# Two decoder layers on one core: later constants, one-step token shift, two-pass sums in RWKV, three-pass LRU gates, whole blocks in the output projections

## The chip, the core and the metric

The kernel runs on one core of a Trainium2 chip. The core has the engines TensorE (PE), VectorE (DVE), ScalarE (ACT), GpSimd (POOL) and SyncE (SP), an on-chip memory of 128 partitions and matmul banks that sum in float32. The metric is the device time of one execution in microseconds (us).

## What is computed

A trunk of two layers on a sequence of T = 256 tokens with D = 2048 columns, in float32. Cut to what matters here:

```python
for layer in range(2):
    h = rms_norm(x, norm_mix[layer])
    if layer == 0:                       # sparse attention beside RWKV-7
        u_nsa, u_rw = split(h @ w_in_a)
        y = concat([nsa(u_nsa), rwkv7(u_rw)]) @ w_out_a
    else:                                # RG-LRU beside HGRN2
        u_lru, u_hg = split(h @ w_in_b)
        y = concat([rglru(u_lru), hgrn2(u_hg)]) @ w_out_b
    x = x + y
    x = x + square(relu(rms_norm(x, norm_mlp[layer]) @ w_ff1)) @ w_ff2

# in rwkv7
u = u + (u_prev - u) * mu                # token shift, u_prev is u one token earlier
kk = k * k_k; kk = kk / max(sqrt(sum over a head's 64 columns of kk*kk), 1e-12)
bonus = (sum over a head's 64 columns of r * k * r_k) * v
# in rglru, for each of 8 blocks of 128 columns
r = sigmoid(xc_block @ wa_block + ba);  i = sigmoid(xc_block @ wx_block + bx)
h_t = a_t * h_(t-1) + b_t                # a from r, b from r, i and xc
y = h * gelu(gate_in)
```

## The kernel before

Activations lie transposed: 16 tiles of 128 columns by 256 tokens. Products are made of float32 values that are cut in two: a rounded high part (type fp32r in the profile) and the rest, the low part. An operand tile holds both beside each other, 512 columns. For each of 16 k, `mm3` (L156) multiplies the high weights with the 512 columns (L163) and the low weights with the 256 high columns (L164); the two halves of the bank are added when it is emptied (`evac`, L175). This pair is called a k below. In the *folded* form the 512 columns are two matmuls of 256 into the same half (L160, L161), so that no adding is left. One 2048 x 128 block of weights times 256 tokens is a *unit*: 16 k.

Weights come as float32 in halves of 8 k (tile `raw`, pool `wraw` with 4 buffers, loads issued by SP in `load`, L135). `split` (L139) makes the high part by a CAST on ACT (`wh`, L141) and the low part by a subtraction on DVE (`wl`, L143); each has 2 buffers in the pool `wspl`.

The program order is: six units of the input projection that run k by k beside each other while x and the weights arrive (tiles `hx_a`, `wh_i_f`, `wl_i_f`; then the mean square `ms_a` with a matrix of ones), then `rwkv_a` with units 6 to 27, the solve, `nsa_head` eight times, the output projection (`mm_o`), the MLP (`mm_f`), and the same with `hgrn_head` and `lru_group` for layer 1. A scheduler sets the order on each engine from the order in which the code is written and from priorities (`tc.high_priority`, `tc.issue_after`).

`con` holds constant matrices (identity, `bones` for sums over 64 rows, `ones`, tables). It is loaded by SP among the loads of the first stage (L283). `out_proj` (L972) goes over one half of the inputs for all 16 output blocks c, and then over the other half in the folded form, after which block c is complete and `touch` (L238) makes the next operand and its sum of squares. In layer 1 the half that comes second is LRU's, whose inputs `ym[0..7]` are the last to be ready: at the end of `lru_group` each of four goes through Exp on ACT (L964), two products, a scan and a product on DVE (L965 to L968), a CAST on ACT (L193) and a subtraction on DVE (L194).

## Time and profile before

| what | value |
|---|---|
| time, median of 3 runs | 2360.75 us (2359.98 to 2374.69) |
| time of the profiled execution | 2360.99 us |
| its span in the trace | 2359.2 us |
| granted TensorE clock, mean | 0.999 |
| first six units, first to last real matmul | 7.16 to 45.5 us |
| output projection, layer 0 | 412.5 to 520 us |
| output projection, layer 1 | 1549.5 to 1645 us |

The profiled execution is 0.24 us above the median and has 1.8 us outside its span. In the rows below a line is the line of the kernel before, `out<-in` the names of the tiles, and square brackets hold the idle time of the engine ahead of the instruction and what ended it. The duration of a matmul overlaps the next one, so the cost of a matmul is the distance between starts.

### The profile page before, as it was taken

To read this page: it belongs to the slowest core of one execution; us is meant where nothing else is said; L and a number is where in the kernel's file an instruction comes from. 1 tells how busy PE (TensorE), PEld (TensorE's weight loads), DVE (VectorE), ACT (ScalarE), POOL (GpSimd) and SP (SyncE) were. 2 spreads that over 40 slices of the span, in tenths; PEclk is the share of its full clock that TensorE was granted. 3 is DMA by queue.
4 is the path that set the end of the run, shared out by engine and by line. 5 is a ranking of instruction groups with operands and counts; after the bars stand their busy time and mean duration, and the time that the engine had idled before them with its cause. 6 is when DMAs were issued, how large, how long until landed. Compare 5 with 4: busy or idle time off the path is not lost.

```text
span 2359.2 us, 38438 instructions
## 1 busy us (share of the span) xinstructions
PE 2349.7 (100%) x14530; PEld 2061.7 (87%) x14530; DVE 1707.4 (72%) x3063; ACT 1252.2 (53%) x2178; POOL 78.6 (3%) x176
## 2 busy tenths in 40 slices
PE   9999999999999999999999999999999999999999
PEld 8888888898888888888888888889888888888888
DVE  6987878777775675675678888788777567567555
ACT  6755467554444444444456665775444444444443
POOL 0112142000000000000000000000000000000000
PEclk9999999999999999999999999999999999999999
DMA  7676754555555555555555444456555555555664
GB/s 245 211 260 230 242 168 137 202 182 192 189 188 192 191 188 189 193 189 188 190 171 181 155 152 153 160 170 215 188 191 191 189 189 191 191 189 189 191 198 137
DMA packets 128296, 445.72 MB, mean 189 GB/s; under 512 B 14960, under 2 KB 21232, under 8 KB 126960
## 3 DMA queue, kind: packets, MB, share of 16 engines
q1 hardware_dynamic: 114768, 407.77, 53.4%
q0 software_dynamic: 8944, 32.00, 4.0%
q10 hardware_dynamic: 4400, 3.50, 0.5%
q8 instruction: 115, 1.88, 0.3%
q14 instruction: 69, 0.57, 0.1%
HBM read 427.99 MB, written 15.20 MB: 188 GB/s over the span
## 4 chain that ended last, share of the span: by engine, by line
PE 83%; DVE 2%; ACT 1%; issue 1%; DMA 0%; POOL 0%; DVEq 0%; ACTq 0%; POOLq 0%
PE mm_f L163 39%; PE mm_f L164 21%; PE mm_i L163 8%; PE mm_i L164 4%; PE mm_o L164 2%; PE mm_o L163 2%; PE mm_o L160 1%; PE mm_o L161 1%; PE hl L872 1%; DVE wl_i L143 1%; DVE wl_o L143 0%; PE psu L541 0%; PE o L752 0%; PE psx L534 0%; ACT wh_o L141 0%
## 5 line engine op out<-in xcount | busy, mean ns | idle before, releaser
L143 DVE TENSOR_TENSOR wl_f<-raw_f,wh_f 128x1024 fp32r<-128x1024 f32 x512 | 627.5, 1226 | 472.2 <-ACT wh_f L141 470.7
L141 ACT CAST wh_f<-raw_f 128x1024 fp32r<-128x1024 f32 x512 | 539.7, 1054 | 758.4 <-PE mm_f L163 559.8
L163 PE MATMUL mm_f<-hx_m,wh_f 128*128 128x512 f32 x2048 | 710.5, 391 | 0.0
L163 PE MATMUL mm_f<-z,wh_f 128*128 128x512 f32 x2032 | 704.7, 391 | 0.0
L164 PE MATMUL mm_f<-hx_m,wl_f 128*128 128x256 f32 x2048 | 573.8, 280 | 0.0
L164 PE MATMUL mm_f<-z,wl_f 128*128 128x256 f32 x2032 | 569.0, 280 | 0.0
L163 PE MATMUL mm_i<-hx_a,wh_i 128*128 128x512 f32 x1440 | 526.1, 403 | 0.2 <-DVE s_r L179 0.2
L163 PEld LDWEIGHTS mm_f<-hx_m,wh_f 128*128 128x128 f32 x2048 | 383.0, 187 | 84.0
L163 PEld LDWEIGHTS mm_f<-z,wh_f 128*128 128x128 f32 x2032 | 380.0, 187 | 83.3
L164 PE MATMUL mm_i<-hx_a,wl_i 128*128 128x256 f32 x1440 | 416.9, 289 | 0.0
L164 PEld LDWEIGHTS mm_f<-hx_m,wl_f 128*128 128x128 f32 x2048 | 387.1, 189 | 0.1
L164 PEld LDWEIGHTS mm_f<-z,wl_f 128*128 128x128 f32 x2032 | 384.0, 189 | 0.0
L163 PEld LDWEIGHTS mm_i<-hx_a,wh_i 128*128 128x128 f32 x1440 | 270.7, 188 | 55.9 <-issue 0.7
L141 ACT CAST wh_i<-raw_i 128x1024 fp32r<-128x1024 f32 x180 | 189.2, 1051 | 176.2 <-PE mm_i L163 152.4
L164 PEld LDWEIGHTS mm_i<-hx_a,wl_i 128*128 128x128 f32 x1440 | 272.1, 189 | 4.8 <-DVE wl_i L143 1.3
L143 DVE TENSOR_TENSOR wl_i<-raw_i,wh_i 128x1024 fp32r<-128x1024 f32 x180 | 220.1, 1223 | 65.2 <-ACT wh_i L141 64.1
L179 DVE TENSOR_TENSOR s_f<-mm_f,t_f 128x256 f32<-128x256 f32 x255 | 106.7, 418 | 0.0
L143 DVE TENSOR_TENSOR wl_o<-raw_o,wh_o 128x1024 fp32r<-128x1024 f32 x64 | 78.3, 1223 | 30.0 <-ACT wh_o L141 29.5
L141 ACT CAST wh_o<-raw_o 128x1024 fp32r<-128x1024 f32 x64 | 67.2, 1050 | 61.2 <-issue 31.1
L178 ACT COPY t_f<-mm_f 128x256 f32<-128x256 f32 x255 | 92.8, 364 | 0.0
L164 PE MATMUL mm_o<-ym,wl_o 128*128 128x256 f32 x256 | 72.7, 284 | 0.9 <-DVE wl_o L143 0.9
L1011 DVE TENSOR_TENSOR s_f<-s_f,rstd_m 128x256 f32<-128x256 f32 x128 | 54.4, 425 | 4.4
(463 smaller groups left out, 2449.7 us busy)
## 6 DMA issues: line engine op xcount, KB each, us to landing
raw_f<-in_w_ff_dram SPq DMA_DIRECT2D x512, 512.0 KB, 4.5
raw_i<-in_w_in_dram SPq DMA_DIRECT2D x180, 512.0 KB, 4.0
raw_o<-in_w_out_dram SPq DMA_DIRECT2D x64, 512.0 KB, 4.4
rwp_d<-rwp POOLq DMA_DIRECT2D x8, 1024.0 KB, 5.4
raw_i_f<-in_w_in_dram SPq DMA_DIRECT2D x16, 384.0 KB, 4.7
pm_d<-pm POOLq DMA_DIRECT2D x8, 512.0 KB, 5.1
cw<-in_cmp_w_dram POOLq DMA_DIRECT2D x2, 2048.0 KB, 17.4
pmc<-pm_d POOLq DMA_DIRECT2D x8, 512.0 KB, 4.5
```

What stands on the lines that cost most here:

```text
L141: A.copy(wh, raw)
L143: V.tensor_sub(wl, raw, wh)
L160: M.matmul(ps[:, :T], wh, mv[:, :T], start=first, stop=False)
L161: M.matmul(ps[:, :T], wh, mv[:, T:], start=False, stop=False)
L163: M.matmul(ps, wh, mv, start=first, stop=False)
L164: M.matmul(ps[:, :T], wl, mv[:, :T], start=False, stop=last)
L178: A.copy(t, ps[:, T:])
L179: V.tensor_add(s, ps[:, :T], t)
L872: M.matmul(pl[:, x * T + i * P : x * T + (i + 1) * P], qk[:, ii], qk[:, ii], start=True, stop=True)
L1011: V.tensor_mul(s, s, rstd)
```

## The change

- `con` loses `ones` (1696 columns to 1568), which is set on the chip, and its load moves behind the loads of unit 6. The load of `par` is cut in two.
- Token shift: u + (u_prev - u) mu is written as u_prev mu + u (1 - mu). The product u (1 - mu) is made on ACT, and one DVE operation is left.
- The two sums over heads in `rwkv_a` (`kss`, `bon`, eight of each) go from one float32 matmul to two in fp32r, with the operand cut in two parts first.
- The LRU gates (16 matmuls) go from float32 to the folded `mm3`; their weights and their operand are cut in two.
- `out_proj` gets a number `nh`: the blocks c >= nh are made whole, 16 k in one bank, between the first halves and the folded halves of the blocks c < nh. It is 8 in layer 0 and 12 in layer 1, so there are 8 + 12 = 20 folded halves in place of 32.
- The reciprocal root for the MLP is placed by hand behind the ninth k of its first unit.

```diff
@@ -36,7 +36,7 @@
 _CON = [
-    ("ident", 128), ("bones", 128), ("ones", 128), ("pair", 128),
+    ("ident", 128), ("bones", 128), ("pair", 128),
     ("ropec", 256), ("ropes", 256), ("reset", 256), ("zd", 256), ("cadd", 32), ("cmul", 32),
@@ -92,7 +92,8 @@
     A.preload_act_table_set(LN_EXP)
-    nc.scalar.dma_start(par, params)
+    nc.scalar.dma_start(par[:, 0:64], params[:, 0:64])
+    nc.scalar.dma_start(par[:, 64:], params[:, 64:])
@@ -102,7 +103,9 @@
-    ident, bones, ones = c_("ident"), c_("bones"), c_("ones")
+    ident, bones = c_("ident"), c_("bones")
+    ones = cst.tile([P, P], F32, name="ones")
+    V.memset(ones, 1.0)
     epst = cst.tile([P, 4], F32, name="epst")
@@ -279,8 +289,6 @@
                         raws.append(raw)
-                        if k == 9:
-                            nc.sync.dma_start(con, consts)
                     for i in range(16):
@@ -306,9 +314,11 @@
                     rstd = rstd_of(acc, "a0", "gc")
+                first.append(unit(w_in0[NFIRST], hx, f"i0_{NFIRST}", tag="gb"))
+                with tc.high_priority(), tc.issue_after(last_load[0].ins):
+                    nc.sync.dma_start(con, consts)
                 A.copy(ones_r, ones)
                 A.copy(bones_r, bones)
-                first.append(unit(w_in0[NFIRST], hx, f"i0_{NFIRST}", tag="gb"))
                 rwkv_a(pa, gate, hx, scaled_by(rstd), rwp_d, pm_d, wts, nb, first, load_cw, anchor)
@@ -335,14 +345,16 @@
         mixed = [None]
+        keep = tl("keep", (P, 28))
+        V.tensor_scalar(keep, p_("mu"), -1.0, 1.0, op0=ALU.mult, op1=ALU.add)
...
             d = tl("d", bufs=2, name=f"d_{name}")
-            V.tensor_sub(d[:rows], ub[:rows, 0:T], ub[:rows, 1:])
-            mixed[0] = V.scalar_tensor_tensor(out[:rows], d[:rows], p_("mu", mu)[:rows], ub[:rows, 1:], ALU.mult, ALU.add)
+            A.activation(d[:rows], ub[:rows, 1:], AF.Copy, scale=keep[:rows, mu : mu + 1])
+            mixed[0] = V.scalar_tensor_tensor(out[:rows], ub[:rows, 0:T], p_("mu", mu)[:rows], d[:rows], ALU.mult, ALU.add)
             return ub
@@ -407,7 +419,10 @@
                 pss = bk_(f"kss_{j}")
-                M.matmul(pss[:, :T], bones, sq, start=True, stop=True)
+                hl = pa.tile([P, 2, T], F32R, tag="hl", name=f"khl_{j}")
+                A.activation(hl[:, 0], k, AF.Square, scale=p_("k_k", j))
+                V.tensor_sub(hl[:, 1], sq, hl[:, 0])
+                sum_over(pss[:, :T], bones_r, hl[:, 0], hl[:, 1])
                 ssm = tl("tm", bufs=2, name=f"ssm_{j}")
@@ -428,7 +443,10 @@
                 psb = bk_(f"bon_{j}")
-                M.matmul(psb[:, :T], bones, rk, start=True, stop=True)
+                hl = pa.tile([P, 2, T], F32R, tag="hl", name=f"bhl_{j}")
+                A.copy(hl[:, 0], rk)
+                V.tensor_sub(hl[:, 1], rk, hl[:, 0])
+                sum_over(psb[:, :T], bones_r, hl[:, 0], hl[:, 1])
                 bv = tl("kf", name=f"bv_{j}")
@@ -761,8 +779,12 @@
             nc.scalar.dma_start(hgmk, hgmask)
-            lw = hp.tile([P, 2, 8, P], F32, name="lw")
-            nc.scalar.dma_start(lw, lru_w)
+            lwh, lwl = (hp.tile([P, 2, 8, P], F32R, name=f"lw{i}") for i in "hl")
+            for w in range(2):
+                raw = wraw.tile([P, 8, P], F32, tag="raw", name=f"raw_lru_{w}")
+                nc.scalar.dma_start(raw, lru_w[:, w])
+                A.copy(lwh[:, w], raw)
+                V.tensor_sub(lwl[:, w], raw, lwh[:, w])
             prm = hp.tile([P, 8, 8], F32, name="prm")
@@ -929,9 +951,11 @@
                     V.scalar_tensor_tensor(x, xb[:, i : i + T], p_("conv_w", 8 * i + j), x, ALU.mult, ALU.add)
+                xhl = hp.tile([P, 2 * T], F32R, tag="xhl", name=f"xhl_{j}", bufs=1)
+                split_to(xhl, x)
                 for w in range(2):
                     ps = bank(f"lru_{j}_{w}", "gb" if w else "ga")
-                    M.matmul(ps[:, 0:T], lw[:, w, j], x, start=True, stop=True)
+                    mm3(ps, lw[0][:, w, j], lw[1][:, w, j], xhl, True, True, True)
                     o = tl("lr" if w == 0 else "li", name=f"lri_{j}_{w}")
@@ -969,23 +993,39 @@
-    def out_proj(xs, w_out, ym, order, acc, hx, gain, name):
-        for o, half in enumerate(order):
-            for c2 in range(8):
-                parts = stream(w_out[half, c2], f"{name}_{half}_{c2}")
-                for x in range(2):
-                    c = 2 * c2 + x
-                    ps = pmm.tile([P, 512], F32, tag="mm", name=f"mm_{name}_{half}_{c}")
-                    wh, wl = parts[x]
-                    for k in range(8):
-                        mm3(ps, wh[:, k], wl[:, k], ym[half * 8 + k], k == 0, k == 7, o == 1)
-                    if o == 0:
-                        s = evac(ps, f"{name}_{half}_{c}")
-                        V.tensor_add(xs[:, c], xs[:, c], s)
-                    else:
-                        with tc.high_priority():
-                            V.tensor_add(xs[:, c], xs[:, c], ps[:, :T])
-                        touch(acc, hx, c, xs[:, c], gain, name)
+    def out_proj(xs, w_out, ym, order, acc, hx, gain, name, nh):
+        touched = []
+        def touch_(c):
+            touch(acc, hx, c, xs[:, c], gain, name, not touched)
+            touched.append(c)
+        def part(half, c):
+            with tc.high_priority():
+                return split(load(w_out[half, c // 2], c % 2, f"{name}_{half}_{c}"), c % 2, f"{name}_{half}_{c}")
+        def halves(todo, c, folded=False):
+            ps = pmm.tile([P, 512], F32, tag="mm", name=f"mm_{name}_{todo[0]}_{c}")
+            n = 8 * len(todo)
+            parts = [part(half, c) for half in todo]
+            for k in range(n):
+                wh, wl = parts[k // 8]
+                mm3(ps, wh[:, k % 8], wl[:, k % 8], ym[todo[k // 8] * 8 + k % 8], k == 0, k == n - 1, folded)
+            return ps
+        for c in range(nh):
+            s = evac(halves(order[:1], c), f"{name}_h_{c}")
+            V.tensor_add(xs[:, c], xs[:, c], s)
+        for c in range(nh, KT):
+            s = evac(halves(order, c), f"{name}_w_{c}")
+            V.tensor_add(xs[:, c], xs[:, c], s)
+            touch_(c)
+        for c in range(nh):
+            ps = halves(order[1:], c, True)
+            with tc.high_priority():
+                V.tensor_add(xs[:, c], xs[:, c], ps[:, :T])
+            touch_(c)
@@ -1000,15 +1040,20 @@
-    def mlp(layer, xs, hx, rstd, nxt, zp, zraw):
+    def mlp(layer, xs, hx, acc, nxt, zp, zraw):
         z = {}
+        rstds = []
...
                 n = f"f1_{layer}_{q}_{k}"
-                s = evac(unit(w_ff1[layer, q * KT + k], hx, n, pool=zraw), n)
-                V.tensor_mul(s, s, rstd)
+                ps = unit(w_ff1[layer, q * KT + k], hx, n, pool=zraw)
+                if not rstds:
+                    with tc.high_priority():
+                        rstds.append(rstd_of(acc, f"m{layer}", after=ninth[0]))
+                s = evac(ps, n)
+                V.tensor_mul(s, s, rstds[0])
                 V.scalar_tensor_tensor(s, s, 0.0, s, ALU.max, ALU.mult)
@@ -1040,26 +1085,24 @@
     acc, hx = norm("m0")
-    out_proj(xs, w_out0, ym, (1, 0), acc, hx, "gmlp0", "o0")
-    rstd = rstd_of(acc, "m0")
+    out_proj(xs, w_out0, ym, (1, 0), acc, hx, "gmlp0", "o0", 8)
     with tc.tile_pool(name="zp0", bufs=2) as zp, tc.tile_pool(name="zraw0", bufs=4) as zraw:
...
                 nacc.extend(norm("a1"))
-            touch(nacc[0], nacc[1], c, xs[:, c], "gmix1", "a1")
-        mlp(0, xs, hx, rstd, next0, zp, zraw)
+            touch(nacc[0], nacc[1], c, xs[:, c], "gmix1", "a1", c == 0)
+        mlp(0, xs, hx, acc, next0, zp, zraw)
     acc, hx = nacc
...
     acc, hx = norm("m1")
-    out_proj(xs, w_out1, ym, (1, 0), acc, hx, "gmlp1", "o1")
-    rstd = rstd_of(acc, "m1")
+    out_proj(xs, w_out1, ym, (1, 0), acc, hx, "gmlp1", "o1", 12)
     with tc.tile_pool(name="zp1", bufs=2) as zp, tc.tile_pool(name="zraw1", bufs=4) as zraw:
-        mlp(1, xs, hx, rstd, lambda c: nc.sync.dma_start(outT[:, c], xs[:, c]), zp, zraw)
+        mlp(1, xs, hx, acc, lambda c: nc.sync.dma_start(outT[:, c], xs[:, c]), zp, zraw)
```

On SP in the first stage stand the loads of x (`xi`), of the raw weights (`raw_i_f`) and of `con`. Before:

```order
L280 DMA raw_i_f_134<-in_w_in_dram 128x768
L280 DMA raw_i_f_136<-in_w_in_dram 128x768
L278 DMA xi_108<-in_xT_dram 128x512
L283 DMA con<-in_consts_dram 128x1696
L280 DMA raw_i_f_139<-in_w_in_dram 128x768
L280 DMA raw_i_f_141<-in_w_in_dram 128x768
```

After, at the end of the first stage's loads:

```order
L290 DMA raw_i_f_157<-in_w_in_dram 128x768
L290 DMA raw_i_f_159<-in_w_in_dram 128x768
L139 DMA raw_i_6_0_498<-in_w_in_dram 128x1024
L139 DMA raw_i_6_1_504<-in_w_in_dram 128x1024
L319 DMA con<-in_consts_dram 128x1568
L139 DMA raw_i_7_0_776<-in_w_in_dram 128x1024
```

The load of `con` has moved behind the whole first stage and both loads of unit 6.

On ACT the cast of `bones` or `ones` out of `con` (`sums`) stands among the casts of weights (`wh_i_f` of the first stage, `wh_i_6_0` and `wh_i_6_1` of unit 6). Before:

```order
L204 ACTIVATE hx_a_1_95<-xi_108,par 128x256
L436 DMA g_1_955<-in_rw_g_dram 128x2x128
L309 CAST sums<-con 128x128
L300 CAST wh_i_f_307<-raw_i_f_136 128x768
L310 CAST sums<-con 128x128
```

After:

```order
L308 CAST wh_i_f_463<-raw_i_f_159 128x768
L144 CAST wh_i_6_0_500<-raw_i_6_0_498 128x1024
L321 CAST sums<-con 128x128
L144 CAST wh_i_6_1_506<-raw_i_6_1_504 128x1024
L187 COPY t_wl<-mm_i_0_112 128x256
```

What ACT has to take out of `con` now stands between the two halves of unit 6.

On ACT in the output projection of layer 1 stand the casts of weights (`wh_o`), the copies that empty a bank (`t_o`), and the last steps of LRU (`lt`, `ym`). Before:

```order
L193 CAST ym_0_13154<-lgt_16476 128x256
L964 ACTIVATE lt_16887<-lt_16887 128x256
L141 CAST wh_o_1_6_1_17298<-raw_o_1_6_1_17296 128x1024
L178 COPY t_o_1_11_17285<-mm_o_1_11_17268 128x256
L141 CAST wh_o_1_7_0_17348<-raw_o_1_7_0_17346 128x1024
L178 COPY t_o_1_12_17319<-mm_o_1_12_17302 128x256
L193 CAST ym_0_13154<-lgt_16592 128x256
```

After:

```order
L202 CAST ym_0_13143<-lgt_16508 128x256
L988 ACTIVATE lt_16940<-lt_16940 128x256
L144 CAST wh_o_1_13_1_17399<-raw_o_1_13_1_17397 128x1024
L202 CAST ym_0_13143<-lgt_16631 128x256
L988 ACTIVATE lt_16944<-lt_16944 128x256
L202 CAST ym_0_13143<-lgt_16754 128x256
L988 ACTIVATE lt_16948<-lt_16948 128x256
L144 CAST wh_o_0_13_1_17405<-raw_o_0_13_1_17403 128x1024
L202 CAST ym_0_13143<-lgt_16877 128x256
```

The four last tiles of LRU (`ym[4]` to `ym[7]`) were spread over the first halves of the blocks; now they stand close together around the casts of block 13.

On PE there, blocks 12 and 13 are interleaved. After:

```order
L167 MATMUL mm_o_1_13_17396<-ym_1_13144,wh_o_1_13_1_17399 128x512
L168 MATMUL mm_o_1_13_17396<-ym_1_13144,wl_o_1_13_1_17401 128x256
L167 MATMUL mm_o_1_12_17343<-ym_0_13143,wh_o_0_12_0_17352 128x512
L168 MATMUL mm_o_1_12_17343<-ym_0_13143,wl_o_0_12_0_17354 128x256
L167 MATMUL mm_o_1_13_17396<-ym_0_13143,wh_o_0_13_1_17405 128x512
L168 MATMUL mm_o_1_13_17396<-ym_0_13143,wl_o_0_13_1_17407 128x256
```

Before, the first k on `ym[0..7]` stood behind all 16 first halves:

```order
L163 MATMUL mm_o_1_15_17380<-ym_1_13155,wh_o_1_7_1_17354 128x512
L164 MATMUL mm_o_1_15_17380<-ym_1_13155,wl_o_1_7_1_17356 128x256
L160 MATMUL mm_o_0_0_17414<-ym_0_13154,wh_o_0_0_0_17404 128x256
L161 MATMUL mm_o_0_0_17414<-ym_0_13154,wh_o_0_0_0_17404 128x256
L164 MATMUL mm_o_0_0_17414<-ym_0_13154,wl_o_0_0_0_17406 128x256
```

The first k on LRU's tiles has moved from behind block 15 to within block 12.

## Rows read from the trace of the kernel before

**Rows 1.** Busy time, share of the span and instructions of each engine.

```profile
PE 2349.7 (100%) x14530; PEld 2061.7 (87%) x14530; DVE 1707.4 (72%) x3063; ACT 1252.2 (53%) x2178; POOL 78.6 (3%) x176
```

**Rows 2.** Stretches: us, busy PE, PEld, DVE, ACT, POOL, PEclk, DMA share, GB/s.

```profile
7.00:20.00 13.00, 13.00 (x75) 11.06 (x74) 10.29 (x18) 8.32 (x13) 0.00 (x0) 1.00 0.93 308
20.00:27.00 7.00, 5.24 (x19) 3.67 (x18) 3.44 (x5) 3.70 (x7) 0.00 (x0) 0.76 0.74 255
60.00:78.00 18.00, 17.57 (x96) 15.18 (x97) 17.83 (x37) 16.15 (x36) 0.59 (x6) 1.00 0.48 160
```

**Rows 3.** Timeline of PE, first stage: start, duration, instruction, idle ahead and releaser.

```profile
21.57 0.50 PE L163 MATMUL mm_i<-hx_a,wh_i_f 128*128 128x512 f32 x1 [1.26 <-ACT wh_i_f L300]
22.57 0.39 PE L164 MATMUL mm_i<-hx_a,wl_i_f 128*128 128x256 f32 x1 [0.49 <-DVE wl_i_f L303]
...
24.18 0.63 PE L163 MATMUL mm_i<-hx_a,wh_i_f 128*128 128x512 f32 x1
...
24.82 0.63 PE L163 MATMUL mm_i<-hx_a,wh_i_f 128*128 128x512 f32 x1
...
33.89 0.28 PE L164 MATMUL mm_i<-hx_a,wl_i_f 128*128 128x256 f32 x1
34.01 0.39 PE L163 MATMUL mm_i<-hx_a,wh_i_f 128*128 128x512 f32 x1
```

**Rows 4.** Timeline of ACT, first stage.

```profile
4.77 0.51 ACT L204 ACTIVATE hx_a<-xi,par 128x256 fp32r<-128x256 f32 x1 [2.75 <-DMA par<-in_params_dram]
5.59 0.83 ACT L300 CAST wh_i_f<-raw_i_f 128x768 fp32r<-128x768 f32 x1 [0.32 <-DMA raw_i_f<-in_w_in_dram]
...
20.29 0.51 ACT L204 ACTIVATE hx_a<-xi,par 128x256 fp32r<-128x256 f32 x1 [3.03 <-DMA xi<-in_xT_dram]
...
24.01 0.30 ACT L309 CAST sums<-con 128x128 fp32r<-128x128 f32 x1 [2.08 <-DMA con<-in_consts_dram]
24.22 0.83 ACT L300 CAST wh_i_f<-raw_i_f 128x768 fp32r<-128x768 f32 x1
```

**Rows 5.** DMA issues of the first 60 us: KB each, median us to landing.

```profile
con<-in_consts_dram SPq DMA_DIRECT2D x1, 848.0 KB, 9.7
```

**Rows 6.** Timeline of PE around the mean square `ms_a`.

```profile
45.53 0.59 PE L217 MATMUL ms_a<-acc_a,con 128*128 128x256 f32 x2
45.77 0.58 PE L163 MATMUL mm_i<-hx_a,wh_i 128*128 128x512 f32 x1
46.19 0.28 PE L164 MATMUL mm_i<-hx_a,wl_i 128*128 128x256 f32 x1
```

**Rows 7.** Instructions of tile mm_o: duration in ns, first and last start.

```profile
L160 PE MATMUL mm_o<-yn,wh_o x128: 283/283/332, 474.2 to 519.9; 128*128 128x256 f32 x128
```

**Rows 8.** Waits of PE from 1540 to 1660 us: total, times, longest.

```profile
PE mm_o L164 <- DVE wl_o L143: 0.9, 2, 0.6
```

**Rows 9.** Timelines of PE and ACT, output projection of layer 1.

```profile
1586.50 0.39 PE L163 MATMUL mm_o<-ym,wh_o 128*128 128x512 f32 x1
...
1589.36 1.06 ACT L141 CAST wh_o<-raw_o 128x1024 fp32r<-128x1024 f32 x1 [1.41 <-PE mm_o L163]
...
1590.58 0.41 ACT L193 CAST ym<-lgt 128x256 fp32r<-128x256 f32 x1
1590.88 0.42 ACT L964 ACTIVATE lt<-lt 128x256 f32<-128x256 f32 x1
...
1601.23 0.41 ACT L193 CAST ym<-lgt 128x256 fp32r<-128x256 f32 x1 [1.75 <-DVE lgt L968]
```

**Rows 10.** Timeline of DVE, output projection of layer 1.

```profile
1586.47 0.42 DVE L966 TENSOR_TENSOR lt<-lt,lri 128x256 f32<-128x256 f32 x1
...
1587.14 0.69 DVE L967 TENSOR_TENSOR_SCAN lxc<-lri,lt 128x256 f32<-128x256 f32 x1
...
1590.45 1.22 DVE L143 TENSOR_TENSOR wl_o<-raw_o,wh_o 128x1024 fp32r<-128x1024 f32 x1 [0.50 <-ACT wh_o L141]
```

**Rows 11.** Timeline of DVE, start of layer 1.

```profile
1234.97 1.23 DVE L143 TENSOR_TENSOR wl_i<-raw_i,wh_i 128x1024 fp32r<-128x1024 f32 x1 [0.49 <-ACT wh_i L141]
```

More of the change, by code (lines that the diff above doesn't have):

```diff
@@ L162, in mm3 @@
         else:
-            M.matmul(ps, wh, mv, start=first, stop=False)
+            ins = M.matmul(ps, wh, mv, start=first, stop=False)
         M.matmul(ps[:, :T], wl, mv[:, :T], start=False, stop=last)
+        return None if folded else ins.ins
+    ninth = [None]
     def unit(src, mv, name, folded=False, tag=None, parts=None, pool=None):
@@ L170, in unit @@
             wh, wl = parts[k // 8]
[L171 removed]
+            ins = mm3(ps, wh[:, k % 8], wl[:, k % 8], mv[k], k == 0, k == KT - 1, folded)
+            if k == 8:
+                ninth[0] = ins
         return ps
```

17 lines of the change are left out of this document (8 added, 9 removed).

## Prediction, made before the result was known

> **What bounds the kernel now.** I read the page's first part first: PE is busy for 2349.7 of 2359.2 us [rows 1]. So PE is the bound, its idle time is under 10 us in all, and a change can move the time only by PE's own instructions and by the few gaps and slow stretches. I then cut the span into stretches and looked for those in which PE's cost per k is above its steady value. The steady value: from 7 to 20 us PE runs 75 matmuls in 13.00 us at clock 1.00 [rows 2], two per k, so 13.00 / 75 x 2 = 0.347 us per k; the low half of it is 34.01 - 33.89 = 0.12 [rows 3]. The stretch from 20 to 27 us stands out: PE idle for 1.76 us and the granted clock at 0.76 [rows 2]. There PE waits 1.26 us for a cast, 0.49 for a subtraction [rows 3], and behind the wait one k takes 24.82 - 24.18 = 0.64 us [rows 3], the lower of the two clock levels (1.2 GHz), until it is back at 2.4 GHz. What released the cast is on ACT: hx_a at 20.29 had waited 3.03 us for a load of x, and a cast out of `con` 2.08 us more [rows 4]. Third come the places that the change touches: the RWKV stretch 60 to 78 us, in which DVE is busy 17.83 of 18 us and ACT 16.15 [rows 2], and the output projection of layer 1, where PE waits 0.9 us for low weights [rows 8]. A measurement of this kernel can tell about 1% (23.6 us) from no change; all terms below are smaller.
>
> **The change part by part**, against the profiled 2360.99 us.
>
> *A, the load of `con` leaves the first stage.* The load ahead of which it stood, x's from k = 8 on, is the one that ACT waits for at 20.29 [rows 4]. `con` is 848 KB [rows 5]; in its place there now stands one more load of x, 128 x 512 float32 or 256 KB, so 592 KB less stand ahead. At the 308 GB/s of this stretch [rows 2] that is 606,000 B / 308 = 1.9 us, so the cast that PE waits for comes at 18.8 and not 20.71, and the wait of 1.26 + 0.49 us goes. The loads two at a time push raw weights of k = 6 back by a load of 256 KB (0.85 us), of which I let 0.4 show; ACT has squares and products of x ahead of the tenth cast now, two or three operations of 0.51 [rows 4], of which 0.8 to 1.1 show. The best case is all of it: 1.26 + 0.49 of waits and five k at the low clock, 5 x (0.64 - 0.35) = 1.45, together -3.2. The worst is 0: another load is late instead. I take -2.0. `par` in two pieces frees hx_a at 4.77, but the cast behind it waits for raw weights until 5.59 anyway [rows 4], so it is worth 0. The memset of `ones` ahead of the warm-up is less than the wait at 20 us that follows it, and costs nothing unless that wait is gone.
>
> *B, the wait for `con` moves.* It now stands on ACT ahead of the second cast of unit 6. The load took 9.7 us from issue to landing [rows 5], and it is issued behind unit 6's own loads; queued behind the waiting cast are the weights of unit 6 and the copies of the first six units. If it lands late, up to 3 us of the old 2.08 + 1.26 come back here; if the 45 us up to then cover it, 0. By its place (loads run four buffers ahead, PE still has some of the first stage and half a unit, 2.8 us, to do) I take +0.5.
>
> *C, sums in two passes.* One float32 matmul of 256 columns costs 0.43 us: the k behind `ms_a` goes 45.77 to 46.19 for its first part where 0.23 is usual, and `ms_a` itself 0.24 [rows 6], 0.24 + 0.19. Two passes cost 2 x 0.12 = 0.234. 16 x (0.43 - 0.234) = -3.1.
>
> *D, the work around it.* DVE loses 28 subtractions and gains 16, ACT gains 28 + 16 operations of 0.42 us [rows 9], 18 us in the 120 us of RWKV's units. In 60 to 78 us ACT has 1.85 us left and DVE 0.17 [rows 2], so the relief on DVE may give PE's idle time there back (18 - 17.57 = 0.43, a bound of -0.5), and ACT, whose casts feed PE, may add delay: some 14 of the 44 operations fall here, 5.9 us against 1.85 us of room, a bound of +4. I take +1.0, near the low end, because the token shift's chain stays as long as it was: one DVE operation becomes one of ACT.
>
> *E, LRU gates.* 16 x (0.43 - 3 x 0.12) = -1.1 on PE. Their weights need two casts and two subtractions at the start of layer 1, and their operand a split, which DVE has room for at 72% [rows 1].
>
> *F, whole blocks.* A folded k costs (519.9 - 474.2) / 127 = 0.360 us [rows 7], a plain one 0.347. 12 halves of 8 k: 96 x 0.013 = -1.25. The Trainium skill, "TensorE: Matmul & The Clock Gate", sections "Back-to-back issue gap" and "LDWEIGHTS (loading the stationary operand)", speaks against this term: it gives N/2.4 + 2.5 ns for N columns and columns/1.2 for a weight load, and by that three matmuls of 256 columns (3 x 109 ns, an estimate) take no longer than one of 512 and one of 256 (216 + 109), so F would be 0 and the whole sum 1.25 us higher. The trace does not agree with it, and the row decides.
>
> *G, output projection of layer 1.* The old waits go: 0.9 [rows 8] and some 0.2 of smaller ones, -1.1. But PE now reaches LRU's tiles within block 12, where before it had 16 first halves to cover them. I laid it out by hand from the start of block 12 (1586.50 [rows 9], called 0). Before PE needs `ym[7]` it has 25 k of other work, 8.7 us. One LRU step is 0.42 (Exp), 0.42, 0.69, 0.42 and 0.41 us [rows 9, 10], 2.4 in all; a cast of weights is 1.06 [rows 9] and a subtraction 1.22 [rows 10]. The cast of block 13's first half waits for the end of block 12's first half at 2.8, so its low part is there at some 5.4 where PE wants it at 4.5: 0.87. `ym[6]` is late by 0.65. The second half of block 13 has buffers only when its first half is done, and its cast shows 0.65 and its subtraction 1.4. Sum +3.6. Layer 0 has no such chain: both inputs are ready.
>
> *H, seams.* Two subtractions of 1.22 [rows 10, 11] stand ahead of the first low weights of layer 1 on DVE; half of one shows, +0.6. At the start of the first MLP the operand of block 7, the last one touched, is needed after 7 k = 2.43 us and takes 1.05 + 1.22 + 0.42 = 2.7: +0.3. The hand-placed root stands where the scheduler already had it, so it is 0.
>
> Sum: -2.0 + 0.5 - 3.1 + 1.0 - 1.1 - 1.25 - 1.1 + 3.6 + 0.6 + 0.3 = -2.55, so 2358.4; the profiled execution is 0.24 above the median, so **2358.2**, which I round to **2358.0**.
>
> **The rivals.**
>
> *R2, all gains and no new waits*: A is -3.2, B, D, H and the new wait of G are 0. -3.2 - 3.1 - 1.1 - 1.25 - 1.1 = -9.75, 2351.0. For it: the scheduler puts the last LRU steps close together, and ACT has idle gaps of 1.41 us between casts there [rows 9]. Against it: the buffers of `wspl` are two, so the casts of block 13 cannot come early.
>
> *R3, slower: LRU's chain keeps its old pace.* Before, the cast of `ym[5]` stands at 1590.58 and that of `ym[7]` at 1601.23 [rows 9], about 5.3 us apart each; the subtraction and its handing on make `ym[7]` whole at 1602.1, 15.6 us behind the start of block 12. PE has 8.6 us of own work, so it would wait 7.0 instead of 3.6, and behind a gap of that kind five k at the low clock cost another 1.5, as they did at 24 us [rows 3]. That is +4.9 on the sum, +2.35, **2363.1**. It decides from where `ym[7]` is later than some 14.4 us behind the start of block 12 (3.4 us more than in my layout would cancel the sum). For it: DVE's order there mixes weights and LRU. Against it: ACT's new order has the four casts together, and the old pace was set by the casts between them.
>
> *R4, the change does not do what it says*: the RWKV stretch is bound by DVE and ACT (17.83 and 16.15 of 18 us [rows 2]), so shorter sums on PE give nothing and C is 0. Then the sum is +0.55, 2361.3.
>
> **How the numbers follow.** Forecast 0.50, R2 0.25, R3 0.15, R4 0.10. R2 and R3 lie at 2351.0 and 2363.1; the range takes both in, with 1.5 us beyond each end for the bounds of B and D (-0.5 below, +3 and +4 above, which do not all come at once): 2349.5 to 2364.5. Every case lies within 1% of 2360.75, so the same has 0.96; 0.02 on either side are left for what no row shows.
>
> **What would show it.** A: no wait of over 1 us and no clock below 1.00 near 20 us, the end of the first stage some 2 us earlier. B: the cast out of `con` with a wait on ACT near unit 6. C: 32 matmuls of 128 x 256 at 0.12. D: PE's busy time and idle gaps from 60 to 100 us. G: waits of PE for `ym`, `wh_o` and `wl_o` within blocks 12 and 13, none for blocks 0 to 11. F: 160 folded k at 0.360. The prediction is wrong if the first stage has its gap elsewhere, or if blocks 12 and 13 run without waits or wait for over 6 us.

## The result and the profile after

| kernel | median (range, executions) | ratio to before (95%) |
|---|---|---|
| before | 2360.84 us (2359.97 to 2376.95, 7) | |
| after | 2381.53 us (2371.62 to 2386.19, 7) | 1.007 (1.0046 to 1.0094) |

The change made the kernel 20.7 us slower; 2358.0 was forecast, and the range ended at 2364.5. The profiled execution of the kernel after took 2384.11 us, its span is 2382.1 us. The first part of its page, as in [rows 1]:

```profile
PE 2365.5 (99%) x14450; PEld 2060.4 (86%) x14450; DVE 1702.4 (71%) x3051; ACT 1271.3 (53%) x2232; POOL 78.7 (3%) x176
```

PE runs fewer instructions, is busy for 15.8 us longer and idle for 7.1 us longer (16.6 against 9.5), so most of the loss of this execution is in matmuls that take longer. I set the first matmul of each stage side by side (us, read from the timelines of PE; *again* is a second profile of the kernel after, unchanged):

| stage, its length | before | after | again |
|---|---|---|---|
| start to `ms_a` (first six units) | 45.53 | 42.62 | 42.90 |
| `ms_a` to output projection 0 | 367.01 | 371.11 | 368.88 |
| output projection 0 | 107.74 | 107.19 | 107.13 |
| MLP 0 | 710.74 | 724.57 | 711.25 |
| mixing of layer 1 | 318.50 | 321.42 | 319.48 |
| output projection 1 | 95.64 | 100.69 | 100.82 |
| MLP 1, to its last matmul | 710.68 | 710.70 | 710.69 |
| span | 2359.2 | 2382.05 | 2364.91 |

There are two losses. One is in MLP 0, a stage in which the change touches nothing behind the first unit: 13.8 us in the one profile, 0.5 in the other. The second is in layer 1, 5 us in the output projection and 1 to 3 ahead of it, in both. The first stage gains 2.6 to 2.9 us against this profile of before, and most of that is gone before the output projection of layer 0.

Not all of the table belongs to the kernels. The 45.53 us are the longest first stage of seven profiles of kernels in which that stage is the old one (the experiments below); the other six have 43.30 to 44.58, median of the seven 43.69. Thirteen with `con` moved have 42.06 to 44.01, median 42.75. So moving `con` is worth some 0.9 us and not 2.9. And the 321.42 us of mixing hold a stretch in which the granted clock is at the lower level, 1.2 GHz, behind a wait of 2.3 us that *again* has as well, without a fall of the clock (319.48). In the kernel after, in the window view that is explained below:

```profile
1553.80:1557.20 3.40, 3.40 (x11) 2.92 (x12) 3.40 (x8) 0.72 (x2) 0.00 (x0) 0.50 0.55 192
```

A like stretch from 314.7 us on, which *again* lacks too, accounts for most of the 2.2 us between the two in the row ahead of output projection 0.

MLP 0 from 530 to 1220 us in the window view (us; busy PE, PEld, DVE, ACT, POOL; PEclk; DMA share; GB/s), in the kernel after:

```profile
530.00:1220.00 690.00, 690.00 (x3908) 598.38 (x3907) 447.39 (x636) 315.86 (x450) 0.00 (x0) 1.00 0.57 186
```

and in its second profile:

```profile
530.00:1220.00 690.00, 690.00 (x3983) 608.40 (x3982) 456.43 (x649) 324.05 (x463) 0.00 (x0) 1.00 0.58 188
```

Both are busy throughout at a granted clock of 1.00, yet the first completes 75 matmuls fewer: 690 / 3908 x 2 = 0.353 us a k against 0.3465. No wait and no clock level tells them apart. Only the duration of the single matmul does, in the view of tile `mm_f` (min/median/max in ns). After:

```profile
L167 PE MATMUL mm_f<-z,wh_f x952: 395/398/403, 702.8 to 1219.7; 128*128 128x512 f32 x191
```

Again:

```profile
L167 PE MATMUL mm_f<-hx_m,wh_f x996: 391/391/391, 529.6 to 1052.1; 128*128 128x512 f32 x200
```

So the same stream of matmuls has a slow cadence (0.353 us a k) and a quick one (0.347), and over MLP 0's 2048 k the difference is 13.8 us. The executions of most kernels here fall into two groups some 14 us apart because of it: of the 20 profiles of this document, the five whose execution lies in an upper group have 724.2 to 724.6 us in MLP 0, and none of the others has more than 718.7. Of 167 executions of the kernel before that were taken beside the result and the experiments, 46 lie above 2372 us; one of the three ahead of the prediction (2374.69 us) did so too.

What answers to [rows 2]:

```profile
7.00:20.00 13.00, 12.37 (x69) 10.21 (x68) 10.43 (x18) 9.01 (x15) 0.00 (x0) 1.00 0.93 289
20.00:27.00 7.00, 6.41 (x35) 5.16 (x34) 6.75 (x13) 7.00 (x13) 0.00 (x0) 1.00 0.87 286
60.00:78.00 18.00, 17.96 (x103) 15.51 (x102) 16.59 (x34) 17.41 (x42) 1.13 (x7) 1.00 0.52 166
```

PE's idle time from 20 to 27 us falls from 1.76 to 0.59 us, with 0.63 ahead of it that were not there, and the clock is 1.00. It is 1.00 there in the other six profiles with the old first stage as well, so the low clock was that of one execution. In 60 to 78 us ACT has become the busier engine of the two. What answers to [rows 4, 5] for `con`, on ACT and among the DMA issues:

```profile
43.41 0.30 ACT L321 CAST sums<-con 128x128 fp32r<-128x128 f32 x1 [1.74 <-DMA con<-in_consts_dram]
...
con<-in_consts_dram SPq DMA_DIRECT2D x1, 784.0 KB, 6.8
```

The waits of PE in the output projection of layer 1 (1566 to 1668 us), as in [rows 8]: total, times, longest.

```profile
PE mm_o L168 <- DVE wl_o L146: 2.7, 4, 1.4
PE mm_o L167 <- DVE ym L203: 0.5, 1, 0.5
PE mm_o L167 <- ACT wh_o L144: 0.2, 1, 0.2
```

and ahead of it (1245 to 1567 us), where PE of the kernel before waits for nothing:

```profile
PE mm_i L167 <- DVE s_lxb L188: 2.3, 1, 2.3
PE mm_i L168 <- DVE wl_i L146: 0.7, 2, 0.3
```

### The profile page after: what moved, and what is told of

The parts are those of the page before. It is cut to its first block, busy times and chain, and to the rows that moved or that the text cites. A ratio compares the mean times of both kernels' runs of the same rounds, so it can differ in the third digit from the quotient of the medians.

```text
span 2382.1 us, 38325 instructions
## 1 busy us (share of the span) xinstructions
PE 2365.5 (99%) x14450; PEld 2060.4 (86%) x14450; DVE 1702.4 (71%) x3051; ACT 1271.3 (53%) x2232; POOL 78.7 (3%) x176
## 4 chain that ended last, share of the span: by engine, by line
PE 83%; DVE 2%; ACT 1%; issue 1%; DMA 1%; POOL 0%; DVEq 0%; POOLq 0%; ACTq 0%
PE mm_f L167 39%; PE mm_f L168 20%; PE mm_i L167 8%; PE mm_i L168 4%; PE mm_o L167 3%; PE mm_o L168 2%; PE hl L894 1%; PE mm_o L164 1%; PE mm_o L165 1%; DVE wl_i L146 1%; DVE wl_o L146 0%; DMA inv<-z_d 0%; PE psu L559 0%; PE o L770 0%; PE psx L552 0%
## 5 line engine op out<-in xcount | busy, mean ns | idle before, releaser
L167 PE MATMUL mm_o<-ym,wh_o 128*128 128x512 f32 x160 | 58.5, 407 | 0.6 <-DVE ym L203 0.5
```

Source lines behind the costliest of these rows:

```text
L167: ins = M.matmul(ps, wh, mv, start=first, stop=False)
```

## Experiments

All were timed in 12 executions each. Since a median is moved by how many fall in the upper group, each is given by the median of its lower group (values within 9 us of its lowest), the number in the upper, and the stages. The lower group of the kernel before lay at 2360.3 to 2361.0 beside every set; one execution of 2857 us and three of the kernel before above 2500 are left out.

### The kernel after again

No edit.

> The kernel after, unchanged, to see how often MLP 0 falls into the slow cadence. Theory 1a (its own timing at ms_m decides, the same in every execution): most executions above 2378. Theory 1b (each kernel falls into either cadence by chance, the kernel before in 7 of 35 executions): most near 2367, a fifth to a third 14 us above.

Lower group 2367.9, 2 of 12 above, ratio 1.002 (0.9996 to 1.0045). So the 20.7 us is mostly the count of executions with the slow cadence in MLP 0: six of the first seven lay at 2380 us or above, 2 of these twelve. What the change does by itself is 7.6 us, the lower group against the 2360.3 of the kernel before beside it. Theory 1a falls, 1b stands.

### What decides the cadence of MLP 0

Ahead of the sum of squares (`delay_acc`), and the place of the root (`root_after_8`, `root_after_13`, and `before_root_after_13`, in which the root is built in the MLP as in the kernel after):

```diff
+if layer == 0:
+    for _ in range(2):
+        V.tensor_scalar(acc, acc, 1.0, 0.0, op0=ALU.mult, op1=ALU.add)
```

```diff
-            if k == 8:
+            if k == 7:    # or 12, in MLP 0 alone
                 ninth[0] = ins
```

> Two DVE operations multiply the sum of squares of the first MLP's norm by one ahead of its root, so PE has to wait for it at the matmul ms_m; nothing else is changed from the kernel after. Theory 1 (cadence): PE runs a k at 0.347 or at 0.353 us, keeps the cadence that it has until an idle gap, and the kernel after went into MLP 0 with the slow one since the wait at ms_m was gone. With a wait there, MLP 0 takes 710.7 us as before and not 724.6, and the time is about 2368. Theory 2 (something that lasts all through MLP 0: where its operands or buffers lie, the order on ACT and DVE, DMA): MLP 0 stays at 724.6, the time at 2381 or a little above.

> The kernel after, but the root's matmul ms_m of MLP 0 stands behind the eighth k of its first unit, not the ninth. PE reaches it 0.35 us earlier, the sum of squares is ready at the old time, so PE waits some 0.2 us there. Theory 1 (cadence): MLP 0 at 0.347 a k, 710.7 us, time 2368. Theory 2: 724.6, 2381.

> The kernel after, but ms_m of MLP 0 stands behind the thirteenth k. The sum of squares is ready long before, no wait. Theory 1: nothing ends the slow cadence, MLP 0 stays at 724.6 and the time at 2381. Theory 2: the same. If it falls to 710.7 all the same, a switch between float32 and fp32r alone decides the cadence, and the wait is not what matters.

> The kernel before, with ms_m of MLP 0 moved from the ninth to behind the thirteenth k of its first unit, so that its wait of 0.17 us for the sum of squares goes. Theory 1: PE comes into MLP 0 with the slow cadence (0.353 in its first 4 us) and keeps it, MLP 0 takes 724.6 in place of 710.7 and the time is 2374.6. Theory 2: what makes MLP 0 slow is not in this kernel, so 710.7 and 2361.

| run | lower group | above | MLP 0 in the profile |
|---|---|---|---|
| delay_acc | 2367.3 | 2 of 12 | 711.76 |
| root_after_8 | 2367.0 | 2 of 12 | 724.22 |
| root_after_13 | 2366.8 | 4 of 12 | 711.73 |
| before_root_after_13 | 2361.4 | 4 of 12 | 710.91 |

Two of the edits did not make the wait that they were to make: in `delay_acc` the scheduler put `ms_m` behind the tenth k, in `root_after_8` the sum of squares is ready in time, and PE is not idle ahead of `ms_m` in either. The wait is in the kernel before, in which `ms_m` starts 0.399 us behind the matmul ahead of it, some 0.16 more than usual.

Neither theory holds as stated. Each of these kernels has both cadences, wherever the root stands, and so has the kernel before with its wait; neither a place in MLP 0 nor the wait decides. What the profiles show is where the cadence can change: the first six k of either MLP take 0.353 each on the mean in all 20 of them, and further on the quick cadence stands in 14 of 20 in MLP 0 and in all 20 in MLP 1. In `before_root_after_13` the slow one lasts for twelve k up to `ms_m` and the quick one begins behind it.

Next, interruptions put in for the test: a float32 matmul of 128 columns within the ninth k of every fourth unit of MLP 0 (`many_draws`, on the kernel after), and in the kernel before one more operation ahead of the root, for a slightly longer wait (`before_longer_wait`).

```diff
             if k == 8:
                 ninth[0] = ins
+                if draws[0] >= 0:
+                    draws[0] += 1
+                    if draws[0] % 4 == 0:
+                        with tc.high_priority(), tc.issue_after(ins):
+                            M.matmul(bank(f"draw_{name}", "gb")[:, :P], ones, ones, start=True, stop=True)
```

```diff
+    V.tensor_scalar(acc[:, 0:1], acc[:, 0:1], 1.0, 0.0, op0=ALU.mult, op1=ALU.add)
     rstd = rstd_of(acc, "m0")
```

> The kernel after with one float32 matmul of 128 columns (ones by ones, its result is used by nothing) behind the ninth k of every fourth unit of MLP 0: 32 in all. Theory 1c (the cadence is drawn anew by chance at each interruption of the stream and kept until the next): MLP 0 shows stretches of 22 us in either cadence, and the times no longer fall into two groups 14 us apart but lie within some 5 us; 32 interruptions of about 0.3 us cost 10, so 711 + 10 and a part of 13.8 for MLP 0. Rival 1d (the cadence belongs to an execution): all stretches of MLP 0 in the same cadence, two groups of times 13 us apart.

> The kernel before with one tiny DVE operation (128 x 1, times one) behind the last addition of the sum of squares ahead of MLP 0, so that PE waits at ms_m somewhat longer than the 0.399 to 0.400 us between starts that stand there now (0.399 was followed by the fast cadence, 0.400 by the slow one; 0.421 to 0.425 at MLP 1 always by the fast one). Theory 1e (the length of the wait decides): MLP 0 fast in all executions, none near 2374. Rival 1c (chance): a fifth to two fifths of them near 2374.

`many_draws`: 2373.7 to 2379.45 in all twelve executions, no second group; MLP 0 takes 718.67, 7.4 us above the 711.25 of the kernel after, 0.23 for each interruption. The stretches in between run at 0.347 a k up to 1217 us; there the slow cadence comes with no other instruction in between, until behind the last interruption, at 1236.06, a k takes 0.347 again. So the cadence does not belong to an execution (1d falls), but it is not drawn evenly at each interruption either (1c): behind all 32 it was the quick one. `before_longer_wait`: 3 of 12 above, 2360.4 below. The edit did not do what it was to do, since in its profile `ms_m` stands one k later and starts 0.241 us behind the matmul ahead of it, so that the wait is gone. The run shows the two groups without a wait; 1e is not tested.

That left the question whether two interruptions do as well. `after_two_draws` is the kernel after with such a matmul in the fourth and the eighth unit alone (`if draws[0] in (4, 8)`):

> The kernel after with two of the small float32 matmuls, behind the ninth k of the fourth and of the eighth unit of MLP 0. Theory (each such interruption takes PE out of the slow cadence, and MLP 0 then keeps the other one): no execution in the upper group near 2381, all within 2365 to 2371. Rival (two are not enough, the cadence behind them is as much a draw as ahead): 2 to 5 of 12 near 2381.

None of 12 was in the upper group (2365.78 to 2372.76, two of them above the 2371 of the theory). Its profile came into MLP 0 with the slow cadence and shows the first interruption; the timeline of PE there (start, us, instruction):

```profile
538.43 0.40 PE L167 MATMUL mm_f<-hx_m,wh_f 128*128 128x512 f32 x1
538.67 0.28 PE L168 MATMUL mm_f<-hx_m,wl_f 128*128 128x256 f32 x1
538.79 0.40 PE L167 MATMUL mm_f<-hx_m,wh_f 128*128 128x512 f32 x1
539.03 0.28 PE L168 MATMUL mm_f<-hx_m,wl_f 128*128 128x256 f32 x1
539.14 0.40 PE L167 MATMUL mm_f<-hx_m,wh_f 128*128 128x512 f32 x1
...
539.73 0.38 PE L187 MATMUL draw_f<-ones 128*128 128x128 f32 x2
539.87 0.37 PE L168 MATMUL mm_f<-hx_m,wl_f 128*128 128x256 f32 x1
540.07 0.40 PE L167 MATMUL mm_f<-hx_m,wh_f 128*128 128x512 f32 x1
540.30 0.28 PE L168 MATMUL mm_f<-hx_m,wl_f 128*128 128x256 f32 x1
540.43 0.39 PE L167 MATMUL mm_f<-hx_m,wh_f 128*128 128x512 f32 x1
540.66 0.28 PE L168 MATMUL mm_f<-hx_m,wl_f 128*128 128x256 f32 x1
540.77 0.39 PE L167 MATMUL mm_f<-hx_m,wh_f 128*128 128x512 f32 x1
```

Ahead of `draw_f` a k takes 538.79 - 538.43 = 0.36 and 0.35, with the 512 columns at 0.40; from 540.43 on it takes 540.77 - 540.43 = 0.34 with 0.39. The interruption took PE out of the slow cadence. It does not keep it out: from 1183 us on this profile has the slow one again, without idle time and without another instruction on PE. In the window view 40 us hold four matmuls fewer:

```profile
1140.00:1180.00 40.00, 40.00 (x233) 34.98 (x232) 26.80 (x38) 21.03 (x34) 0.00 (x0) 1.00 0.59 193
1188.00:1228.00 40.00, 40.00 (x229) 34.71 (x228) 28.23 (x43) 21.82 (x35) 0.00 (x0) 1.00 0.45 147
```

Eight of the 20 profiles change so in the last 50 us of MLP 0, seven to the slow cadence and `root_after_8` to the quick one. All eight are among the nine of kernels with the new gates, and in seven the change comes 3.1 to 3.5 us behind the issue of a load of gate weights (`raw_lru`, L785 of the kernel after). Whether that load is the cause was not tried; the cost is at most 1 us, since little of MLP 0 is left.

### Layer 1: gates and whole blocks, each alone and left out

`layer1_halves` is the kernel after with `nh` 16 in layer 1; `gates_one_pass` the kernel after with the old gates; `old_layer1` both; `gates_only` and `blocks_only` put one of the two edits (blocks in both layers) into the kernel before.

```diff
-    out_proj(xs, w_out1, ym, (1, 0), acc, hx, "gmlp1", "o1", 12)
+    out_proj(xs, w_out1, ym, (1, 0), acc, hx, "gmlp1", "o1", 16)
```

```diff
-                split_to(xhl, x)
-                    mm3(ps, lw[0][:, w, j], lw[1][:, w, j], xhl, True, True, True)
+                    M.matmul(ps[:, 0:T], lw[:, w, j], x, start=True, stop=True)
```

> The kernel after with no whole blocks in layer 1's output projection (nh 16, halves in the old order). Theory: PE's waits within blocks 12 and 13 (3.4 us) and the lower clock behind them make that stage 100.7 us in place of 95.6; without them it is 95.7 and the fast executions are 5 us quicker than those of the kernel after, 2362. Rival: the stage lost because the LRU chain ends later through the added splits; then it stays above 98 with halves as well, and the time at 2365 or more.

> The kernel after with the LRU gates as before (one float32 matmul each, no splits of weights and operand). Theory: the wait of 2.3 us of mm_i for s_lxb, an emptying on DVE that stands behind the added splits, goes, and so do the waits for low weights at the start of layer 1; the layer's mixing stage falls from 319.6 to 321.4 to some 318.5, the fast executions to 2364.5. Rival: the wait is one of DVE's other work, the stage gains nothing but loses 1.1 us of PE time, 2368.

> The kernel before with the LRU gates in three passes (weights and operand cut in two), nothing else. Theory: the splits stand on DVE and ACT, which the mixing stage of layer 1 keeps busy for 84% and 67% of its time, and delay the LRU chain, which reaches into the output projection: the mixing stage 319 to 321 us in place of 318.5, the output projection 98.5 in place of 95.6, fast executions at 2364. Rival: the prediction's term E, 1.1 us less on PE and the splits hidden: 2360.

> The kernel before with the new output projection (whole blocks from 8 on in layer 0, from 12 on in layer 1), nothing else. Theory: layer 0's stage 0.6 us shorter, layer 1's 2.3 longer (98.0) by waits in blocks 12 and 13, MLP 0 0.3 to 0.5 longer by the operand of block 7: fast executions at 2362.5. Rival: waits only come with the LRU splits; 2359.

> The kernel after with the LRU gates as before and halves in layer 1's output projection: what is left of the change is con, shift, sums and whole blocks in layer 0. Theory: gates and whole blocks account for all that layer 1 lost, so mixing stage 318.5 to 319, output projection 95.6, fast executions 2360 to 2361, no quicker than the kernel before, as what the first stage won is given back by the solve. Rival: layer 1's loss is in part of another origin (the order that follows from the rest); output projection above 97, time above 2363.

| run | mixing | output projection 1 | lower group | above |
|---|---|---|---|---|
| before, for comparison | 318.50 | 95.64 | 2360.3 to 2361.0 | |
| gates_only | 321.41 | 98.77 | 2366.6 | 3 of 12 |
| blocks_only | 318.91 | 97.94 | 2362.6 | 0 of 12 |
| layer1_halves | 320.85 | 98.78 | 2365.9 | 2 of 12 |
| gates_one_pass | 319.06 | 97.96 | 2362.8 | 3 of 12 |
| old_layer1 | 319.20 | 95.77 | 2361.7 | 7 of 12 |

The gates cost 3.1 us in the output projection, the whole blocks 2.3, both together 5.2 (100.82), neither 0.1. That the two add up so closely is in part chance: five of the seven profiles with all edits have 3.4 us at a granted clock of 0.50 in that stage, which the runs with one alone lack; `many_draws`, with both and a clock of 1.00 throughout, takes 99.86. For `layer1_halves` the rival was right, since the gates' share stays. The gates, which save matmul time, are the most expensive edit of layer 1: 5.7 us alone by the lower groups. The waits of PE in `gates_only` from the start of layer 1 to the end of its output projection:

```profile
PE mm_i L163 <- DVE s_lxb L179: 2.2, 1, 2.2
PE mm_o L164 <- DVE wl_o L143: 0.9, 2, 0.8
PE mm_i L164 <- DVE wl_i L143: 0.6, 2, 0.3
PE mm_o L160 <- DVE xs L993: 0.5, 1, 0.5
PE mm_o L160 <- ACT wh_o L141: 0.4, 1, 0.4
```

Those of `mm_i` go when the gates are taken out (`gates_one_pass`, `blocks_only`). What `s_lxb` stands behind is on DVE; in the kernel after, where PE is idle from 1551.4 to 1553.7:

```profile
1550.39 1.22 DVE L146 TENSOR_TENSOR wl_i<-raw_i,wh_i 128x1024 fp32r<-128x1024 f32 x1
1551.53 0.42 DVE L203 TENSOR_TENSOR ym<-lgt,ym 128x256 fp32r<-128x256 f32 x1
1551.86 0.42 DVE L990 TENSOR_TENSOR lt<-lt,lri 128x256 f32<-128x256 f32 x1
1552.20 0.41 DVE L339 TENSOR_TENSOR lgt<-s_lgt,rstd_a 128x256 f32<-128x256 f32 x1
1552.53 0.68 DVE L991 TENSOR_TENSOR_SCAN lxc<-lri,lt 128x256 f32<-128x256 f32 x1
1553.13 0.40 DVE L188 TENSOR_TENSOR s_lxb<-mm_i,t_lxb 128x256 f32<-128x256 f32 x1
```

The emptying of a bank that PE needs stands behind a low weight and four LRU operations. A like row stands ahead of `s_lxb` at 1534.51 us in the kernel before, where PE does not wait for it. That the splits make the row later against PE's stream is read from this; what the runs show is that the wait comes and goes with the gates. Behind it the granted clock falls to 0.50 for 3.4 us in five of the nine profiles with the gates, and the mixing takes 320.9 to 321.5 us there, 319.5 to 320.0 in the other four.

The 3.1 us in the output projection are only in part waits: PE is idle there for 2.1 us in `gates_only`, 1.1 in the kernel before. The rest is mostly the gates' own matmuls, which come later: 22 of 48 stand in this stage and take 3.1 us, in the kernel before 8 of 32 with 1.4 (a float32 matmul shows as two).

### The first part of the program

`con_only`, `sums_only` and `shift_only` put one edit each into the kernel before (the lines of the diff above); `con_and_blocks0` has `con` moved and whole blocks in layer 0 alone.

> The kernel before with the load of con moved behind unit 6, ones set on the chip and par in two pieces, nothing else. Theory: the first stage ends 3 us earlier (ms_a at 42.6 in place of 45.5), and nothing takes it back but a wait for con near unit 6 that PE does not see: fast executions at 2358. Rival: what was won is lost again in the RWKV stretch, which is bound by DVE and ACT, so the first unit of the output projection starts where it did, 412.5, and the time is 2360.5.

> The kernel before with the two sums of RWKV's first part in two passes, nothing else. Theory: what a float32 matmul costs beyond two passes is a switch back to fp32r, 0.19 us, and only those of kss went (8), since bon stood ahead of other float32 matmuls, and lora now stands alone 4 times more: the stretch up to the norm of the keys (nr_k at 240.9) at most 1 us shorter, time 2360 to 2361. Rival: the prediction's term C, 16 switches or 3.1 us shorter: nr_k at 237.8.

> The kernel before with the token shift by one operation of ACT and one of DVE in place of two of DVE, nothing else. Theory: neither engine's load decides, nr_k within 0.7 us of 240.9, time 2360 to 2361.5. Rival: the casts behind ACT's 28 added operations feed PE late, the upper bound of the prediction's term D: 2363 or more.

> The kernel before with con moved and whole blocks in layer 0 alone (from 8 on), the two edits that showed no loss by themselves. Theory: -0.6 in layer 0's output projection, -1 at its start, +0.3 in MLP 0: fast executions at 2359.5, 1 us below the kernel before. Rival: the edits do not add up, since each changes the order of the rest, and it is 2361 or more.

| run | `ms_a` | `nr_kc` | output projection 0 | lower group | above |
|---|---|---|---|---|---|
| before | 45.53 | 240.90 | 412.54 | 2360.3 to 2361.0 | |
| con_only | 42.52 | 238.70 | 411.53 | 2360.6 | 4 of 11 |
| sums_only | 43.69 | 237.51 | 418.10 | 2371.8 | 1 of 12 |
| shift_only | 44.29 | 243.44 | 416.69 | 2369.1 | 6 of 12 |
| con_and_blocks0 | 42.66 | | 409.54 | 2359.8 | 2 of 12 |
| again (all edits) | 42.90 | 238.95 | 411.78 | 2367.9 | 2 of 12 |

`nr_kc` is the norm of the compressed keys; the expectations call it `nr_k`. `con_only`: against the one profile of before the first stage ends 3.0 us earlier, 2.2 is left at `nr_kc` and 1.0 at the output projection. But the median of seven profiles with the old first stage is 43.69, and five with nothing changed up to the output projection start it between 410.06 and 412.54, median 412.3; three with `con` moved and nothing else up to there have a median of 411.3. So some 0.9 is gained and some 1.0 is left, and a loss in between is not shown. The solve does wait, in that run for

```profile
PE psu L544 <- ACT xv L539: 1.0, 1, 1.0
PE psh L522 <- DVE zat L519: 0.7, 1, 0.7
```

but such waits come without the edit too: from `nr_kc` to the output projection PE is idle for 2.8 us in `blocks_only`, in which `con` has not moved, and for 1.0 in `con_and_blocks0`, in which it has. By the time the rival was the nearer one. `sums_only` is 1.6 us quicker from `ms_a` to `nr_kc` (193.8 against 195.4), between the two expectations, and then loses far more in places that it does not touch: PE is idle for 9.5 us from there to MLP 0, 1.5 in the kernel before. The largest wait is for an emptying on DVE in the output projection of layer 0:

```profile
PE mm_o L163 <- DVE s_o L179: 4.3, 1, 4.3
```

Behind it the granted clock is at 0.50 until 448.8 us, and a k takes 0.64 there. `shift_only` takes 199.2 from `ms_a` to `nr_kc`, 3.8 more, but PE is idle for less of it (0.55 us against 0.91). The loss is in 128 matmuls of 64 rows (`pair`) that the edit does not touch. Their share of 46 to 240 us in the window view (PE, PEld, DVE, then as above), in the kernel before and in `shift_only`:

```profile
46.00:240.00 194.00, 13.68 (x128) 11.96 (x128) 10.65 (x16) 1.00 0.70 233
46.00:240.00 194.00, 17.61 (x128) 14.93 (x128) 10.98 (x16) 1.00 0.68 227
```

In the kernel before 26 of them are followed by the next matmul within 0.06 us, in `shift_only` 5, and most of the others take 0.11. In the kernel after `pair` takes 16.45 us. Why they no longer start beside each other was not tried.

Both expectations on the whole time missed. By the lower groups the five parts alone come to 0.3 + 10.9 + 8.2 + 5.7 + 1.6 = 26.7 us, and all of them together to 7.6; `old_layer1`, with con, sums, shift and blocks of layer 0, to 1.4. The edits do not add up; as `sums_only` and `shift_only` show, an edit moves waits and the order of matmuls in places that it does not touch. The 4.3 us of `s_o` are gone in the kernel after, most of the loss in `pair` is not. Why `sums` and `shift` cost so little once they are together was not tried.

### A version without the upper group

`con_and_blocks0` with the two interruptions in MLP 0:

> con moved and whole blocks in layer 0 alone, on the kernel before, with the two small float32 matmuls in MLP 0 as well. Theory: no execution in the upper group near 2373; all within 2358 to 2363, so a median 1 us and a mean some 5 us below the kernel before. Rival: 2 to 5 of 12 near 2373.

All 12 executions lie within 2359.27 to 2362.41 us, median 2360.13, mean 2360.3; the kernel before beside them has a lower group at 2360.6 and 4 of 22 above, mean 2363.5 without one outlier. The ratio is 0.999 (0.9977 to 1.0004), so the medians are not told apart, but the upper group is gone.

## Why the prediction was wrong

**The step that failed first is one that was not taken: the cost of a k was put at 0.347 us wherever PE is busy.** The 0.347 was taken from 13 us of the first stage and carried over to 2048 k of MLP 0. The profile of before had both cadences, even at the head of MLP 0: its first eight k, from 520.28 to 523.11 us, took 0.354 each, and those behind `ms_m` 0.347. I did not look at that, nor at the execution of 2374.69 us among the three. 13.8 of the 20.7 us are this. The change moved the sum of squares and put a wait of 0.3 us at the operand of block 7, but the experiments do not show that this makes the slow cadence likelier: 2 of 12 on repetition against 46 of 167 before. Why six of the first seven executions had it stays open.

Without it the kernel after is 7.6 us slower, and the forecast of 2.8 us quicker is still wrong in sign. Term by term:

- **A** (-2.0, bound -3.2): -2.6 to -3.0 against the profile from which it was worked out, but only some -0.9 between the medians of seven and thirteen profiles. It was mis-sized because it was read off one execution, the slowest in this stage: the low clock at 24 us, for which the bound counts 1.45, is in none of the other six. (606,000 / 308 is 2.0 us and not 1.9, which changes little.)
- **B** (+0.5): ACT waits 1.74 us for `con` at 43.41; from `ms_a` to `nr_kc` `con_only` loses 0.8, `con_and_blocks0` 0.1.
- **C** (-3.1): mis-sized, -1.6 in `sums_only`. The price of float32 is 0.19 us at the switch back to fp32r, and I counted a switch for each of 16 sums. In the kernel before the switch of `bon` is not there, since other float32 matmuls follow it; eight of `kss` went, and four of `lora` came since `lora` now stands alone. That is 0.7 us; where the rest of the 1.6 comes from was not traced.
- **D** (+1.0, bound +4): +3.8 by itself, the size of the bound, but not by its mechanism. PE is not idle for longer; `pair` takes 3.9 us more. With all edits together, from `ms_a` to `nr_kc`, B, C and D are +0.7 to +1.1.
- **E** (-1.1 on PE, splits hidden) is **the term with the wrong sign**: +5.7 by itself. I took room on DVE from 72% over the whole span [rows 1]; in layer 1's mixing it is 85%, and the splits were not hidden. In mixing and output projection together `gates_only` loses 6.0 us: PE is idle for 3.7 us more, most of it ahead of `s_lxb`, and 3.4 us at half the clock cost 1.7. The LRU chain ends later: the last gate matmul stands 18 us behind the start of the output projection in the kernel after, 7 us in the kernel before.
- **F** (-1.25): the price of a folded k stands, 0.360 (96 of them from 1633.0 to 1667.2 us). Layer 0 gained 0.6 of its 0.8; layer 1's part cannot be read apart from G.
- **G** (-1.1 + 3.6 = +2.5): the sum is right, +2.3 in `blocks_only`, but with two misses that cancel, so that is luck. The old waits do not go: ahead of block 12, where none was forecast, PE still waits for `wl_o`, 0.8 us at 1578.0 and 0.2 at 1591.3. Within blocks 12 and 13, from 1605.7 us on, the waits are 2.4 and not 3.6 (0.4, 0.5, 0.2 and 1.4).
- **H** (+0.6 + 0.3): 0.3 of waits for `wl_i` at the start of layer 1, half of the forecast, and 0.3 for the operand of block 7, as forecast.

Rival R3 had the sign and 2363.1. Of its mechanism, LRU's old pace, the waits do not show the 7 us (PE waited 2.4 within blocks 12 and 13), but the low clock behind them, which it priced at 1.5, was there: 0.50 from 1618.6 to 1622.0 us. R4, that C is nothing, was nearer for the front of the program than C's -3.1.

## What to carry to other kernels

Where one engine is busy throughout, look at the cost of one step of its stream in every stage and in several executions, before the waits: here 6 ns in 347, held for 2000 steps, outweighed every edit. A saving on the busiest engine that puts work on a chain of other engines has to be weighed where that chain ends, with the load of that stage and not of the span. With a scheduler, one edit alone says little of its share in a set: five parts cost 26.7 us one by one and 7.6 together. And a gap or a low clock in one profile may be that execution's own: the stage from which A was worked out took 43.3 to 45.5 us in seven profiles without any edit to it.

## What was unexpected in the hardware

PE runs pairs of a 512-column and a 256-column fp32r matmul in two lasting cadences at the same granted clock of 1.00: 0.3465 and 0.353 us a pair. In MLP 0 of before (from `ms_m` on) and of after it kept one of them for 700 us, but it can change with nothing else on PE, as in eight of 20 profiles near the end of MLP 0. A float32 matmul of 128 columns in between, at 0.23 us, was followed by the quicker one each time, in two of the profiles out of the slower one, and 0 of 36 executions with such interruptions lay in the upper group, against 46 of 167 of the kernel before. `ms_m`, a float32 matmul of 256 columns, does not do so each time: in 6 of 20 profiles the slow cadence goes on behind it in MLP 0. What in the engine holds the cadence no run shows.

The other surprise is `pair`: the same 128 matmuls of 64 rows took 13.68 us in the kernel before, where 26 of them are followed within 0.06 us, and 17.61 in `shift_only`, where 5 are.
